# Other start addresses for the split weights and for every tile behind them, in a one-core decoder block

## The chip, the cores and the metric

The kernel runs on one core of one Trainium2 chip. The metric is the device time of one execution in microseconds (us); the times before the change are given as the median of three runs.

## The reference

One decoder block for 256 tokens of width 2048, in float32: a per-channel shift, scale and gate from `c`, a mixer made of sparse attention (NSA) beside a state-space layer (S5), and then a layer of 16384 single-neuron experts (PEER) of which each token uses 16 in each of 8 heads. Cut to what matters here:

```python
h = rms_norm(x, norm_mix_g[i]) * (1.0 + sc1) + sh1
proj = h @ w_in[i]
...
mixed = ga * (o_attn @ w_up_attn[i]) + gb * (y @ w_up_ssm[i])
x = x + g1 * (mixed @ w_out[i])
h2 = rms_norm(x, norm_ffn_g[i]) * (1.0 + sc2) + sh2
x = x + g2 * peer(h2, peer_w_q[i], peer_sub_keys[i], peer_u[i], peer_v[i])
```

In `peer`, the products of `h2` with `peer_u` are called the first expert products here, and those of the gated result with `peer_v` the second. The kernel forms both for all experts and gives the unused ones a gate of zero.

## The kernel before

**Split products.** Every large product is made of three float32r products. `load_split` (lines 95 to 101) loads a block of 128 x 1024 weights into `st`, ScalarE copies it, rounded, to `hi` (line 98), and VectorE writes the rest `st - hi` to `lo` (line 100). The activations are split in the same way by `split` (lines 103 to 105) into the two halves of a tile: `cat` for the projections (`hcat`), for `w_out` (`mcat`) and for queries and first expert products (`h2`); `ycat`, `y2cat` and `ocat` for the smaller products; `wcat` for the second expert products. Then `hi*hi`, `hi*lo` and `lo*hi` are summed in PSUM.

```python
    def load_split(src):
        st = load(src)
        hi = stream.tile([P, 1024], FR, name="hi", bufs=3)
        S.activation(hi, st, AF.Copy)
        lo = stream.tile([P, 1024], FR, name="lo", bufs=3)
        V.tensor_sub(lo, st, hi.bitcast(F32))
        return hi, lo
```

**Which operand stands still.** In the stages with lines 431 to 433 (`first_columns`, the first 24 blocks of `w_in`) and 512 to 514 (`pair_T`: the rest of `w_in`, `glu_w`, `w_up_ssm`, `w_up_attn`, the query weights and `peer_u`) a slice of 128 columns of `hi` or `lo` is loaded into the array, and 256 columns of the activations (`cat`, `ycat`, `y2cat` or `ocat`) move through it: 24 matmuls a load. In the stages with lines 529 to 531 (`cols_t`: `w_v` and `w_out`) and 1180 to 1182 (`v_cols`: `peer_v`) it is the other way round: 128 columns of `cat` or `wcat` are loaded, and 512 columns of `hi` or `lo` move: 12 matmuls a load. Of the 738 loads, 48 go to `first_columns`, 394 to `pair_T`, 40 to `cols_t` and 256 to `v_cols`.

```python
                    PE.matmul(pt[:, e], wh, c[:, 0], start=(k == 0), stop=False)
                    PE.matmul(pt[:, e], wh, c[:, 1], start=False, stop=False)
                    PE.matmul(pt[:, e], wl, c[:, 0], start=False, stop=(k == n - 1))
```

Each matmul loads its own 128 columns first; the load for the next matmul runs while this one's columns move (engines PEld and PE in the profile).

**Order.** `tick` mixes the small work (modulation vectors, S5, attention, top-16 searches) into the loads by tables of how many loads have gone by. The expert stage then goes through 16 groups of 8 expert blocks: per group 32 loads of `peer_v` and the `peer_u` products of the next group between them.

**Where tiles lie.** Pools take a row of each partition one behind the other: `const`, `stream`, `big`, then the pool of the stage. In `stream` these are five buffers of `st`, three of `hi`, three of `lo` (4096 bytes each); in `big` the tile `pad` (line 177, 48 floats) and `cat`; behind them `pa` or `pb` with all others. A tile named `t8` (`ycat`, `y2cat`, `ocat` and others) is 8256 bytes long, so that the next begins 64 bytes further modulo 512; a buffer of `wcat` (line 1161) is 8320 bytes long, so that the three are 128 bytes apart modulo 512. A buffer is taken by turns: the loads use `hi` and `lo` number 0, 1, 2, 0, and so on.

Of the kernel before, what the change touches and what calls it, by code (L numbers as in the profile page):

```python
# [11 lines left out]
F32 = mybir.dt.float32  # L12
FR = mybir.dt.float32r
# [7 lines left out]
P = 128  # L21
# [51 lines left out]
def hybrid_block(ctx: ExitStack, tc: tile.TileContext, i: dict, out: bass.AP):  # L73
# [4 lines left out]
    stream = ctx.enter_context(tc.tile_pool(name="stream", bufs=3))  # L78
    big = ctx.enter_context(tc.tile_pool(name="big", bufs=1))
# [10 lines left out]
    def load(src):  # L90
        st = stream.tile([P, 1024], F32, name="st", bufs=5)
        nc.sync.dma_start(st, src)
        return st

    def load_split(src):
        st = load(src)
        hi = stream.tile([P, 1024], FR, name="hi", bufs=3)
        S.activation(hi, st, AF.Copy)  # L98
        lo = stream.tile([P, 1024], FR, name="lo", bufs=3)
        V.tensor_sub(lo, st, hi.bitcast(F32))  # L100
        return hi, lo

# [71 lines left out]
        for tb in range(TB):  # L174
            V.tensor_scalar(dst[tb], xt[tb], r[:, tb:tb + 1], None, op0=OP.mult)

    big.tile([P, 48], F32, name="pad")

    def new_cat():
        return big.tile([P, KD, 2, SEQ], FR, name="cat")  # L180
# [266 lines left out]
    def stage(sn, order=None, after=None):  # L447
        ks, units, steps = stages[sn]
        sl = slice(ks[0], ks[-1] + 1)
        V.scalar_tensor_tensor(a1[:, sl], modT[:, 16 + ks[0]:17 + ks[-1]], 1.0, par("norm_mix_g")[:, sl],  # L450
                               op0=OP.add, op1=OP.mult)
        for k in ks[::2]:
            modulate_T(hcat, k, [t[:, 0] for t in xn], a1, modT[:, 0:16], mm_bank)
        for n, u in enumerate(order or range(len(units))):
            for step in steps[len(steps) * n // len(units):len(steps) * (n + 1) // len(units)]:
                step()
            if (sn, n) == (2, 0):
                bias_load()
            if (sn, n) == (2, 6):
                make_table(0)  # L460
            if (sn, n) == (3, 0):
                bias_rows()
            w = i["w_first0"][sn, u] if sn < 2 else i["w_first"][sn - 2, u]
            first_columns(*load_split(w), ks, units[u])
            if after:
                after(n)
# [34 lines left out]
    def pair_T(blocks, cat, kh):  # L501

        pt = mm_bank()
        for e, srcs in enumerate(blocks):
            n = len(srcs) * kh
            for h, src in enumerate(srcs):
                hi, lo = load_split(src)
                for kk in range(kh):
                    k = h * kh + kk
                    c = at(cat, k)  # L510
                    wh, wl = hi[:, kk * P:(kk + 1) * P], lo[:, kk * P:(kk + 1) * P]
# [3 lines that stand above are left out]
                tick()  # L515
        return pt

    def cols_t(srcs, cat, emit):

        pts = [ps_bank() for _ in range(TB)]  # L520
        for c, src in enumerate(srcs):
            hi, lo = load_split(src)
            for tb in range(TB):
                for kk in range(2):
                    k = 2 * c + kk
                    wh, wl = hi[:, kk * 512:(kk + 1) * 512], lo[:, kk * 512:(kk + 1) * 512]
                    sh = cat[:, k, 0, tb * P:(tb + 1) * P]
                    sl = cat[:, k, 1, tb * P:(tb + 1) * P]
                    PE.matmul(pts[tb], sh, wh, start=(k == 0), stop=False)
                    PE.matmul(pts[tb], sh, wl, start=False, stop=False)  # L530
                    PE.matmul(pts[tb], sl, wh, start=False, stop=(k == 2 * len(srcs) - 1))
            tick()
        for tb in range(TB):
            emit(tb, pts[tb])
# [833 lines left out]
```

## Time and profile before

| what | value |
|---|---|
| median of 3 runs | 2552.22 us (2546.16 to 2557.81) |
| the profiled execution's own time | 2554.16 us |
| its span, first to last instruction | 2552.1 us |
| PE busy, share of the span | 96% |
| weight loads (PEld) busy | 83% |
| VectorE busy | 65% |
| ScalarE busy | 46% |
| mean granted TensorE clock | 0.981 |

The busy share of PE counts a matmul from its start to its modelled end. Matmuls overlap in the array, so that the next one starts long before the end of this one; the time that a row of matmuls takes is read from start to start, and the duration of one is longer than that by the way through the array.

### The profile page before, as it was taken

Reading aid. Unit: us, or ns where it says so; the run is one execution under the profiler, and the core shown is the slowest. Engines: PE = TensorE matmul, PEld = TensorE weight load, DVE = VectorE, ACT = ScalarE, POOL = GpSimd, SP = SyncE. Lnnn points to the kernel's source line nnn. Section 1 sums busy time; section 2 is a strip of 40 time slices with the busy share of each in tenths; the row PEclk is TensorE's granted clock in tenths of the full one; section 3 lists DMA queues with packets and bytes.
Section 4 is the critical chain, followed back from the end, with each engine's and each line's share of the span. In section 5 each row is a group of like instructions: output and inputs, shape, how many; then the busy total and the mean of one; then the engine's idle time right before and its main releaser. Section 6 shows DMA issues by size and latency. Waiting matters only on the chain.

```text
span 2552.1 us, 42825 instructions
## 1 busy us (share of the span) xinstructions
PE 2448.5 (96%) x17410; PEld 2127.0 (83%) x17410; DVE 1668.6 (65%) x2690; ACT 1176.5 (46%) x1527; POOL 65.1 (3%) x117
## 2 busy tenths in 40 slices
PE   7999999999999999995599999999999999999997
PEld 4787787777898788995488999999899999989996
DVE  4559767886555579959555665666666566665666
ACT  4444524645534534456444444444444444444444
POOL 0000200000000000000100000000000000000000
PEclk9999999999999999996799999999999999999999
DMA  9965666666777677554756665665666566565554
GB/s 347 376 227 176 225 202 210 214 199 209 281 264 255 211 237 253 188 186 173 298 197 192 211 198 197 203 208 191 203 206 207 192 204 206 191 207 189 190 191 139
DMA packets 149761, 552.03 MB, mean 216 GB/s; under 512 B 16748, under 2 KB 20492, under 8 KB 147133
## 3 DMA queue, kind: packets, MB, share of 16 engines
q1 hardware_dynamic: 135200, 493.08, 57.1%
q0 software_dynamic: 8928, 40.17, 4.4%
q10 hardware_dynamic: 5436, 16.06, 1.8%
q8 instruction: 136, 2.23, 0.4%
q14 instruction: 61, 0.49, 0.1%
HBM read 526.12 MB, written 23.12 MB: 215 GB/s over the span
## 4 chain that ended last, share of the span: by engine, by line
PE 57%; DVE 5%; DMA 2%; ACT 1%; issue 1%; DVEq 0%; POOL 0%; POOLq 0%; ACTq 0%
PE mm L512 10%; PE mm L513 10%; PE mm L514 10%; PE ps L1182 9%; PE ps L1180 9%; PE ps L1181 9%; DVE o L1120 1%; DVE o L1122 1%; DMA st<-in_peer_w_q_dram 1%; DVE lo L100 1%; DVE o L1118 1%; DMA gm<-gt_dram 0%; ACT hi L98 0%; PE ps L1004 0%; DMA gt_dram<-stage 0%
## 5 line engine op out<-in xcount | busy, mean ns | idle before, releaser
L100 DVE TENSOR_TENSOR lo<-st,hi 128x1024 fp32r<-128x1024 f32 x738 | 902.2, 1223 | 667.9 <-ACT hi L98 666.8
L98 ACT ACTIVATE hi<-st 128x1024 fp32r<-128x1024 f32 x738 | 781.4, 1060 | 1120.3 <-PE mm L513 430.5
L512 PE MATMUL mm<-cat,hi 128*128 128x256 f32 x2832 | 804.1, 284 | 0.6 <-ACT cat L104 0.6
L513 PE MATMUL mm<-cat,hi 128*128 128x256 f32 x2832 | 793.8, 280 | 1.0 <-DVE cat L105 0.9
L514 PE MATMUL mm<-cat,lo 128*128 128x256 f32 x2832 | 792.8, 280 | 0.0
L512 PEld LDWEIGHTS mm<-cat,hi 128*128 128x128 f32 x2832 | 533.6, 188 | 33.4 <-issue 26.5
L514 PEld LDWEIGHTS mm<-cat,lo 128*128 128x128 f32 x2832 | 539.6, 191 | 1.6 <-issue 0.8
L513 PEld LDWEIGHTS mm<-cat,hi 128*128 128x128 f32 x2832 | 533.5, 188 | 5.9 <-issue 2.4
L1180 PE MATMUL ps<-hi,wcat 128*128 128x512 f32 x1024 | 401.7, 392 | 21.0 <-ACT wcat L104 21.0
L1182 PE MATMUL ps<-hi,wcat 128*128 128x512 f32 x1024 | 403.0, 394 | 0.2 <-DVE wcat L105 0.2
L1181 PE MATMUL ps<-lo,wcat 128*128 128x512 f32 x1024 | 401.3, 392 | 0.0
L1180 PEld LDWEIGHTS ps<-hi,wcat 128*128 128x128 f32 x1024 | 193.1, 189 | 60.7 <-ACT wcat L104 21.1
L1182 PEld LDWEIGHTS ps<-hi,wcat 128*128 128x128 f32 x1024 | 192.9, 188 | 46.4 <-DVE wcat L105 4.8
L1181 PEld LDWEIGHTS ps<-lo,wcat 128*128 128x128 f32 x1024 | 193.2, 189 | 40.6
L431 PE MATMUL ps<-cat,hi 128*128 128x256 f32 x384 | 110.9, 292 | 0.5 <-ACT hi L98 0.5
L433 PE MATMUL ps<-cat,lo 128*128 128x256 f32 x384 | 106.8, 284 | 1.0 <-DVE lo L100 1.0
L432 PE MATMUL ps<-cat,hi 128*128 128x256 f32 x384 | 107.3, 281 | 0.1
L222 PE MATMUL ps<-st,sct 128*32 128x256 f32 x960 | 88.8, 390 | 0.4 <-DMA st<-in_ada_w_dram 0.4
L431 PEld LDWEIGHTS ps<-cat,hi 128*128 128x128 f32 x384 | 72.7, 190 | 16.0 <-issue 12.6
L1128 PE MATMUL ps<-o,o 128*128 128x128 f16 x512 | 49.5, 281 | 38.1 <-DVE o L1120 38.0
L1128 PEld LDWEIGHTS <-o 128*128 128x128 f16 x512 | 46.5, 159 | 41.0 <-DVE o L1120 40.8
L433 PEld LDWEIGHTS ps<-cat,lo 128*128 128x128 f32 x384 | 71.9, 190 | 4.5 <-DVE lo L100 2.0
(353 smaller groups left out, 2606.3 us busy)
## 6 DMA issues: line engine op xcount, KB each, us to landing
st<-in_peer_u_dram SPq DMA_DIRECT2D x256, 512.0 KB, 4.0
st<-in_peer_v_dram SPq DMA_DIRECT2D x256, 512.0 KB, 4.2
st<-in_ada_w_dram SPq DMA_DIRECT2D x136, 512.0 KB, 4.4
st<-in_w_in_dram SPq DMA_DIRECT2D x66, 512.0 KB, 4.0
ada_w<-in_ada_w_dram SPq DMA_DIRECT2D x28, 1024.0 KB, 9.5
st<-in_w_first_dram SPq DMA_DIRECT2D x48, 512.0 KB, 6.0
st<-in_w_out_dram SPq DMA_DIRECT2D x32, 512.0 KB, 4.0
st<-in_peer_w_q_dram SPq DMA_DIRECT2D x32, 512.0 KB, 4.3
```

The costliest lines, as they stand in the source:

```text
L98: S.activation(hi, st, AF.Copy)
L100: V.tensor_sub(lo, st, hi.bitcast(F32))
L431: PE.matmul(pt[:, e], hi[:, cs], hcat[:, k, 0], start=first, stop=False)
L432: PE.matmul(pt[:, e], hi[:, cs], hcat[:, k, 1], start=False, stop=False)
L433: PE.matmul(pt[:, e], lo[:, cs], hcat[:, k, 0], start=False, stop=end)
L512: PE.matmul(pt[:, e], wh, c[:, 0], start=(k == 0), stop=False)
L513: PE.matmul(pt[:, e], wh, c[:, 1], start=False, stop=False)
L514: PE.matmul(pt[:, e], wl, c[:, 0], start=False, stop=(k == n - 1))
L1128: PE.matmul(pt[:, tt], o1[:, part, :, h0 + tt], o2[:, h0 + tt], start=(part == 0), stop=(part == 1))
L1180: PE.matmul(pts[tb], wc[:, 0, ts], vh, start=(eb == 0), stop=False)
L1181: PE.matmul(pts[tb], wc[:, 0, ts], vl, start=False, stop=False)
L1182: PE.matmul(pts[tb], wc[:, 1, ts], vh, start=False, stop=(eb == GRP - 1))
```

## The change

The tiles `hi` and `lo` get 32 bytes more (8 floats, not used); one tile `gap` of 416 bytes, not used, is taken between the first `hi` and the first `lo`; and `pad` shrinks from 192 to 160 bytes.

```diff
+    gaps = {}
+
     def load_split(src):
         st = load(src)
-        hi = stream.tile([P, 1024], FR, name="hi", bufs=3)
+        hi = stream.tile([P, 1024 + 8], FR, name="hi", bufs=3)[:, :1024]
         S.activation(hi, st, AF.Copy)
-        lo = stream.tile([P, 1024], FR, name="lo", bufs=3)
+        if "gap" not in gaps:
+            gaps["gap"] = stream.tile([P, 104], F32, name="gap", bufs=1)
+        lo = stream.tile([P, 1024 + 8], FR, name="lo", bufs=3)[:, :1024]
         V.tensor_sub(lo, st, hi.bitcast(F32))
         return hi, lo
...
-    big.tile([P, 48], F32, name="pad")
+    big.tile([P, 40], F32, name="pad")
```

No instruction is added, removed or moved: the built programs hold the same instructions in the same order on each engine, with the same waits and the same shapes, and only addresses differ. All tiles behind `lo` lie 576 bytes further (64 modulo 512). Start of the tiles in a partition, in bytes modulo 512, from the built programs:

| tile | before | with the change |
|---|---|---|
| `st`, 5 buffers | 0 | 0 |
| `hi`, buffers 0, 1, 2 | 0, 0, 0 | 0, 32, 64 |
| `lo`, buffers 0, 1, 2 | 0, 0, 0 | 0, 32, 64 |
| `cat` | 192 | 256 |
| `wcat`, buffers 0, 1, 2 | 0, 128, 256 | 64, 192, 320 |
| `ycat`, two tiles | 0, 448 | 64, 0 |
| `y2cat`, two tiles | 64, 128 | 128, 192 |
| `ocat`, two tiles | 256, 320 | 320, 384 |
| `xs`, `sq`, `acc` | 0 | 64 |

Slices that matmuls take of these tiles begin a multiple of 512 bytes after the tile's start, so the table holds for them too.

## Rows read from the trace of the kernel before

**Rows 1.** The page's parts 1 and 4: TensorE's busy time, share of the span and instructions; and the shares of the span in the chain that ended last, by engine.

```profile
PE 2448.5 (96%) x17410; PEld 2127.0 (83%) x17410; DVE 1668.6 (65%) x2690; ACT 1176.5 (46%) x1527; POOL 65.1 (3%) x117
...
PE 57%; DVE 5%; DMA 2%; ACT 1%; issue 1%; DVEq 0%; POOL 0%; POOLq 0%; ACTq 0%
```

**Rows 2.** Busy time of each engine in four stretches of the span (start and end in us, length; then busy us and instructions of PE, weight loads, DVE, ACT and POOL; granted TensorE clock; DMA share; GB/s). The first three hold all that stands ahead of the expert stage (the third is mostly the gate matrices), the last is the expert stage.

```profile
0.00:1000.00 1000.00, 968.60 (x7624) 780.89 (x7625) 667.83 (x1494) 456.53 (x725) 46.12 (x92) 0.99 0.70 243
1000.00:1150.00 150.00, 146.79 (x1277) 145.79 (x1275) 117.69 (x225) 74.59 (x88) 0.52 (x1) 1.00 0.58 190
1150.00:1250.00 100.00, 45.11 (x448) 42.35 (x448) 77.03 (x57) 56.06 (x59) 6.99 (x11) 0.68 0.51 206
1250.00:2552.00 1302.00, 1287.99 (x8064) 1157.97 (x8064) 806.02 (x917) 589.29 (x658) 11.50 (x13) 0.99 0.60 199
```

**Rows 3.** Groups of instructions of the whole run by line and shape: line, engine, operation, out<-in, shapes, count, then busy us, mean ns of one, and the idle time before them with what ended it.

```profile
L100 DVE TENSOR_TENSOR lo<-st,hi 128x1024 fp32r<-128x1024 f32 x738 | 902.2, 1223 | 667.9 <-ACT hi L98 666.8
L512 PE MATMUL mm<-cat,hi 128*128 128x256 f32 x2832 | 804.1, 284 | 0.6 <-ACT cat L104 0.6
...
L98 ACT ACTIVATE hi<-st 128x1024 fp32r<-128x1024 f32 x738 | 781.4, 1060 | 1120.3 <-PE mm L513 430.5 <-PE ps L1182 288.8 <-issue 100.1
...
L431 PE MATMUL ps<-cat,hi 128*128 128x256 f32 x384 | 110.9, 292 | 0.5 <-ACT hi L98 0.5
```

**Rows 4.** Who waited for whom over the whole run (us in total, times, longest).

```profile
ACT hi L98 <- PE mm L513: 430.5, 260, 4.6
ACT hi L98 <- PE ps L1182: 288.8, 191, 2.1
```

**Rows 5.** Groups of TensorE in the expert stage alone, 1250 to 2552 us; columns as in rows 3.

```profile
L514 PE MATMUL mm<-cat,lo 128*128 128x256 f32 x1664 | 464.6, 279 | 0.0
...
L1181 PE MATMUL ps<-lo,wcat 128*128 128x512 f32 x1024 | 401.3, 392 | 0.0
```

**Rows 6.** The same for 1000 to 1150 us, the queries and the first expert products.

```profile
L513 PE MATMUL mm<-cat,hi 128*128 128x256 f32 x395 | 110.9, 281 | 0.0
```

**Rows 7.** The same for 350 to 600 us, the projections.

```profile
L513 PE MATMUL mm<-cat,hi 128*128 128x256 f32 x402 | 112.4, 280 | 0.0
```

**Rows 8.** TensorE's instructions in order of time, 1391 to 1397 us (start us, us, engine, line, operation, out<-in, shapes, count): the first and the last of 48 matmuls of an expert product that follow each other without a gap.

```profile
1391.34 0.28 PE L512 MATMUL mm<-cat,hi 128*128 128x256 f32 x1
...
1396.66 0.28 PE L514 MATMUL mm<-cat,lo 128*128 128x256 f32 x1
```

**Rows 9.** The same view, 1479 to 1485 us: the first and the last of 48 matmuls of a later expert product.

```profile
1479.04 0.28 PE L512 MATMUL mm<-cat,hi 128*128 128x256 f32 x1
...
1484.57 0.28 PE L514 MATMUL mm<-cat,lo 128*128 128x256 f32 x1
```

**Rows 10.** The groups of TensorE in 1391.4 to 1396.6 us and in 1479.1 to 1484.5 us (one row of each, in this order), columns as in rows 3.

```profile
L513 PE MATMUL mm<-cat,hi 128*128 128x256 f32 x16 | 4.4, 276 | 0.0
...
L513 PE MATMUL mm<-cat,hi 128*128 128x256 f32 x16 | 4.5, 281 | 0.0
```

**Rows 11.** TensorE in order of time, 757.6 to 759.1 us, in the product with `w_up_attn`: the first matmul on `ocat`'s first tile and the first on its second tile, 12 intervals later.

```profile
757.62 0.29 PE L512 MATMUL mm<-ocat,hi 128*128 128x256 f32 x1
...
759.06 0.28 PE L512 MATMUL mm<-ocat,hi 128*128 128x256 f32 x1
```

**Rows 12.** The same view, 756.3 to 757.5 us: two matmuls on `ocat`'s second tile, ten intervals apart.

```profile
756.32 0.28 PE L513 MATMUL mm<-ocat,hi 128*128 128x256 f32 x1
...
757.50 0.28 PE L514 MATMUL mm<-ocat,lo 128*128 128x256 f32 x1
```

**Rows 13.** The same view, 631.2 to 633.1 us, in the product with `glu_w`: a matmul on `ycat`'s first tile, the first on its second tile (five intervals later), and the twelfth on that.

```profile
631.24 0.28 PE L513 MATMUL mm<-ycat,hi 128*128 128x256 f32 x1
...
631.84 0.29 PE L512 MATMUL mm<-ycat,hi 128*128 128x256 f32 x1
...
633.11 0.28 PE L514 MATMUL mm<-ycat,lo 128*128 128x256 f32 x1
```

**Rows 14.** The same view, 1339.1 to 1346.9 us, second expert products on the `wcat` buffers at 0 and 256: two matmuls 34 intervals apart.

```profile
1339.13 0.39 PE L1180 MATMUL ps<-hi,wcat 128*128 128x512 f32 x1
...
1346.84 0.39 PE L1181 MATMUL ps<-lo,wcat 128*128 128x512 f32 x1
```

**Rows 15.** The same view, 1347.5 to 1352.5 us, on the `wcat` buffer at 128: two matmuls 21 intervals apart.

```profile
1347.54 0.40 PE L1181 MATMUL ps<-lo,wcat 128*128 128x512 f32 x1
...
1352.42 0.40 PE L1181 MATMUL ps<-lo,wcat 128*128 128x512 f32 x1
```

**Rows 16.** The same view, 1438.6 to 1440.5 us, on the `wcat` buffer at 256 just after TensorE had stood still (the row ahead of these lasts 0.50 us): two matmuls eight intervals apart.

```profile
1438.62 0.40 PE L1180 MATMUL ps<-hi,wcat 128*128 128x512 f32 x1
...
1440.49 0.40 PE L1182 MATMUL ps<-hi,wcat 128*128 128x512 f32 x1
```

**Rows 17.** The same view, 800 to 803.2 us, in the product with `w_out`: two matmuls 14 intervals apart.

```profile
799.97 0.39 PE L529 MATMUL ps<-hi,cat 128*128 128x512 f32 x1
...
803.17 0.39 PE L531 MATMUL ps<-hi,cat 128*128 128x512 f32 x1
```

**Rows 18.** The splits into `wcat` on ScalarE and VectorE, whole run, columns as in rows 3.

```profile
L105 DVE TENSOR_TENSOR wcat<-xs,wcat 128x512 fp32r<-128x512 f32 x64 | 43.3, 685 | 2.2 <-ACT wcat L104 2.2
...
L104 ACT ACTIVATE wcat<-xs 128x512 fp32r<-128x512 f32 x64 | 39.7, 625 | 24.2 <-DVE xs L1159 20.7 <-PE ps L1182 3.4
```

## Prediction

> **What bounds the kernel now.** I began with the busy shares and the chain that ended last: TensorE is busy for 96% of the span, and its matmuls are the largest part of the chain by far [rows 1]. By stretches that holds nearly everywhere: 969 of the first 1000 us, 147 of the 150 us after, 1288 of 1302 us in the expert stage; only from 1150 to 1250 us, where the gate matrices are built, is TensorE idle for half the time, and almost none of the split products lie there [rows 2]. Who waits for whom says the same from the other side: ScalarE's rounding of the weights waits for matmuls to give a buffer back, 430 and 289 us in total [rows 4]. So the end is set by how closely matmuls follow each other, and the change, which alters addresses alone, can act only through that, or through the work of other engines on the moved tiles.
>
> The next view is the order of time on TensorE, read from start to start. Matmuls of the same form, with no gap between them, run at several steady rates:
>
> - 256 columns, moving from `cat` (192) against `hi` and `lo` (0): 48 matmuls start within 1391.34 to 1396.66 us, 47 intervals of 113.2 ns [rows 8]; another product of the same kind takes 47 intervals of 117.7 ns from 1479.04 to 1484.57 us [rows 9]. The mean duration is 276 ns in the one and 281 ns in the other [rows 10], so a duration is the interval plus 163 ns. That lets me read intervals from mean durations.
> - 256 columns, moving from `ocat`'s first tile (256) against weights at 0: 12 intervals take 1.44 us, 120.0 ns each [rows 11]; from its second tile (320): 118.0 ns [rows 12].
> - 256 columns, moving from `ycat`: 120.0 ns on the tile at 0; on the tile at 448 the first eleven intervals take 1.27 us, 115.5 ns each [rows 13].
> - 512 columns from `hi` and `lo` (0) against `wcat`: 226.8 ns on the buffers at 0 and 256 [rows 14], 232.4 ns on the buffer at 128 [rows 15]; on the one at 256, right after TensorE had stood still, 233.8 ns [rows 16].
> - 512 columns against `cat` (192): 228.6 ns [rows 17].
>
> I put these in order by one number, the start of the moving tile less that of the stationary one, modulo 256, and call it the distance. Then 0 and 256 give the same 120.0, 64 and 320 about 118, and 192 and 448 both can reach about 113. With 512 columns, distance 0 gives 226.8 while its rhythm lasts. This order is my reading of the rows; they show it only for multiples of 64.
>
> **The change part by part.** *Other engines.* VectorE's subtraction takes 1223 ns for 1024 columns, ScalarE's copy 1060 ns [rows 3]; the same operations with 512 columns into `wcat`, which lies at 0, 128 and 256, take 685 and 625 ns [rows 18], so the further 512 columns cost 1.05 and 0.85 ns each and the start of the output shows no price of its own. I cost the moved outputs at nothing. The cover is that both engines wait for TensorE [rows 4] and are busy for 65% and 46% of the span [rows 1]. If VectorE's 738 subtractions became 100 ns longer, the 74 us would still fit into its idle 35%. `st`, which the weight loads write, does not move.
>
> *256 columns against `hi` and `lo`.* `cat` goes to 256, the weights to 0, 32 and 64 by turns: distances 0, 224 and 192, each for 24 matmuls. Distance 0 has its row: 120.0 ns, entry included [rows 11]. For 192 I take what `ycat` shows on entry from distance 0, 1.27 us for eleven intervals [rows 13], and 113.2 ns for the other 13: 114.3 ns. Distance 224 has no row. It lies between 192 and 0, so it is bounded by 113.2 and 120.0; I take 117.2, a little above the middle, since it is entered from 0 each time. The mean is (120.0 + 117.2 + 114.3) / 3 = 117.2 ns. Now it is 279 - 163 = 116 ns for the 4992 matmuls of the expert stage [rows 5], 281 - 163 = 118 ns for some 1190 between 1000 and 1150 us [rows 6], and about 117 ns for the other 3470 on `cat`, taken from the projections' 280 [rows 7]. That gives 4992 x 1.2 = +6.0 us, 1190 x -0.8 = -1.0 us and 3470 x 0.2 = +0.7 us: **+5.7 us**. The 960 matmuls on `ycat`, `y2cat` and `ocat` change places among the same prices: 0, with 3 us either way.
>
> *512 columns against `wcat`.* The moving tile is at 0, 32 or 64 now, `wcat` at 64, 192 or 320. For the two buffers at 64 and 320 the distances are 192, 224 and 0, for the one at 192 they are 64, 96 and 128. Each load has 12 matmuls and then the distance changes, so the rhythm of 226.8 ns that now lasts over loads and buffers [rows 14] is broken every time. I bound the first two buffers by 226.8 and by the 233.8 after a break [rows 16] and take the middle, 230.3; for the third I take the middle of 228.6 [rows 17] and 232.4 [rows 15], 230.5. The mean, 230.4, stands against 392 - 163 = 229 ns now [rows 5]: 3072 x 1.4 = **+4.3 us**. The 480 matmuls of `cols_t` get distances 0, 32 and 64 in place of one price of 228.6; bounded by 226.8 and 233.8, I take +1 ns: **+0.5 us**.
>
> The sum is +10.5 us on the profiled execution's 2554.2 us. That execution is 1.9 us above the median of the runs, so on the median I forecast 2552.2 + 10.5 = 2562.7, say **2563 us**. TensorE being the bound, none of it is hidden except between 1000 and 1250 us.
>
> *The bounds of the sum.* Lowest: 192 and 224 at 113.2, 0 at 120.0, mean 115.5: 4992 x -0.5 - 1190 x 2.5 - 3470 x 1.5 = -10.7 us; 512 columns at (2 x 226.8 + 228.6) / 3 = 227.4: -4.9 us; the small terms -4 us; together -20 us, 2533 us. Highest: all 256-column matmuls at 120.0: 4992 x 4 + 1190 x 2 + 3470 x 3 = +33 us; 512 columns at 233.8: +15 us; small terms +5 us; together +53 us, 2605 us.
>
> **A rule that says otherwise.** The rows show one and the same instruction at 113.2, 117.7 and 120.0 ns on tiles that differ in where they start [rows 8, 9, 11]. The Trainium skill, "TensorE: Matmul & The Clock Gate", section "Step-by-step: what each phase is for", has it that TensorE reads moving and stationary operands through two independent ports, and that loading the next weights takes nothing from the running matmul. By that rule the addresses would not matter, and the change would cost nothing; the trace does not agree as far as these rates go. I keep it as a rival.
>
> **The rivals.**
>
> *No effect, 2552 us.* The rates could belong to something else than the start addresses: 113.2 and 117.7 ns occur at one and the same pair of addresses [rows 8, 9], and so do 226.8 and 233.8 [rows 14, 16]. Then the mixture stays as it is and the sum is 0. Against it: the buffer at 128 and the tiles at 256 have prices of their own [rows 11, 15]. Chance 0.16.
>
> *Slower: the rhythm is lost everywhere.* The mechanism is that a fast rate needs one distance for many loads, as in rows 8 and 14, and a shift by 32 after each load prevents it. Then 192 stays at 117.7, 224 costs 120.0 as 0 does, mean 119.2: 4992 x 3.2 + 1190 x 1.2 + 3470 x 2.2 = +25 us; `wcat` at (2 x 233.8 + 230.5) / 3 = 232.7: 3072 x 3.7 = +11.4 us; `cols_t` +1.5 us. Together +38 us, 2590 us. With the other terms as forecast, this side begins (over 0.5%, 12.8 us, about what a measurement of this kernel can tell from no change) where distance 224 costs more than some 118 ns. For it: the rate after a break [rows 16]. Against it: `ycat` falls to its fast rate within a load [rows 13]. Chance 0.21.
>
> *Faster: the shifts break the slow rhythm instead.* If each new distance throws the matmuls into the fast rate, as rows 13 show for one, all of them would come to about 114 ns: 4992 x -2 - 1190 x 4 - 3470 x 3 = -25 us, and -5 us from 227.4 ns on `wcat`: 2522 us. Against it: `ocat` at distance 0 keeps 120.0 ns [rows 11], and 0 is the distance of every third load. Chance 0.13.
>
> **How the numbers follow.** The forecast, a mixture, has 0.50: +10.5 us with some 10 us either way, so about 0.33 of it within 0.5% and 0.17 slower by more. With no effect (0.16) that makes 0.49 within, 0.17 + 0.21 = 0.38 slower, 0.13 faster. The range goes from 2540 us (20 us above the faster rival's middle) to 2584 us (most of the way to the slower rival): what lies outside are most of the faster rival and the upper half of the slower one, some 0.2.
>
> **What would show it.** In the order of time, loads on `hi` number 0 should run at 120 ns against `cat`, those on number 2 near 114 ns, with number 1 between; the mean duration of line 514 in the expert stage should be near 280 ns (279 now), that of line 1181 near 393 (392 now), and no long stretch at 389. ScalarE's and VectorE's durations should stay at 1060 and 1223 ns. The prediction is wrong if intervals below 113 or 226 ns appear, for no row here has them; if the rates do not follow the buffer's number; or if ScalarE or VectorE becomes what matmuls wait for.

## The result, and the profile after

The kernel with the change takes 2577.79 us (median of four runs, 2576.32 to 2581.93) against 2550.76 us for the kernel before in the runs beside it (2546.16 to 2557.81): ratio 1.0106, 95% interval 1.0079 to 1.0133, 27 us slower. The forecast was 2563 us with 2540 to 2584 around it. So the time lies in the range and the sign of the sum was right, but the sum, +10.5 us, was two and a half times too small, and the case "slower by over 0.5%", which came true, had had 0.38.

The page's busy times and the shares of the chain that ended last, against [rows 1]:

```profile
PE 2479.9 (96%) x17410; PEld 2146.6 (83%) x17410; DVE 1669.2 (65%) x2690; ACT 1177.3 (46%) x1527; POOL 64.9 (3%) x117
...
PE 57%; DVE 5%; DMA 2%; ACT 1%; issue 1%; DVEq 0%; POOL 0%; SPq 0%; ACTq 0%; POOLq 0%
```

Only TensorE's column moved: +31.4 us for the same 17410 matmuls, and +19.6 us of weight loads beside them. The profiled execution's span is 2579.9 us against 2552.1. The four stretches, with the columns of [rows 2] (the first three have the same bounds; the last is the expert stage again, to the later end):

```profile
0.00:1000.00 1000.00, 970.60 (x7563) 782.39 (x7564) 662.19 (x1460) 455.98 (x723) 45.93 (x92) 1.00 0.70 242
1000.00:1150.00 150.00, 149.99 (x1273) 148.10 (x1271) 119.45 (x255) 68.82 (x80) 0.52 (x1) 1.00 0.59 193
1150.00:1250.00 100.00, 51.33 (x514) 48.07 (x512) 81.12 (x59) 63.66 (x67) 6.98 (x11) 0.67 0.46 190
1250.00:2580.00 1330.00, 1308.00 (x8064) 1168.03 (x8064) 806.48 (x918) 588.81 (x658) 11.48 (x13) 0.99 0.60 197
```

The granted clock is what it was in every stretch, within 0.01. The expert stage holds the same 8064 matmuls and costs 1308.0 - 1288.0 = 20.0 us more. The other 11.4 us of busy time lie ahead of it, where the first 1000 us now see 61 matmuls fewer get done. Of the 31.4 us the span shows 27.8; the other 3.6 us were taken in by time in which TensorE stood idle.

The groups behind that, with the columns of [rows 3, 5]: first VectorE's and ScalarE's work on the moved tiles (whole run; what were lines 100, 98, 105 and 104).

```profile
L104 DVE TENSOR_TENSOR lo<-st,hi 128x1024 fp32r<-128x1024 f32 x738 | 902.6, 1224 | 684.4 <-ACT hi L100 678.8 <-PE ps L795 3.7 <-PE mm L518 1.3
...
L100 ACT ACTIVATE hi<-st 128x1024 fp32r<-128x1024 f32 x738 | 782.1, 1061 | 1144.2 <-PE mm L517 453.4 <-PE ps L1186 264.5 <-issue 141.6
...
L109 DVE TENSOR_TENSOR wcat<-xs,wcat 128x512 fp32r<-128x512 f32 x64 | 43.4, 685 | 2.3 <-ACT wcat L108 2.3
...
L108 ACT ACTIVATE wcat<-xs 128x512 fp32r<-128x512 f32 x64 | 39.2, 617 | 24.7 <-DVE xs L1163 21.2 <-PE ps L1186 3.4
```

Then TensorE in the expert stage:

```profile
L518 PE MATMUL mm<-cat,lo 128*128 128x256 f32 x1664 | 467.5, 281 | 0.0
...
L1185 PE MATMUL ps<-lo,wcat 128*128 128x512 f32 x1003 | 395.9, 395 | 0.0
```

And in the projections, 350 to 600 us, and in the queries and first expert products, 1000 to 1150 us (one row of each view):

```profile
L517 PE MATMUL mm<-cat,hi 128*128 128x256 f32 x392 | 110.7, 283 | 0.0
```
```profile
L517 PE MATMUL mm<-cat,hi 128*128 128x256 f32 x410 | 115.4, 282 | 0.0
```

The outputs on shifted addresses cost the other engines nothing: 1224 and 1061 ns for 1223 and 1060, 685 for 685. TensorE's matmuls are longer everywhere: in the expert stage 279 became 281 and 392 became 395 [rows 5], in the projections 280 became 283 [rows 7], between 1000 and 1150 us 281 became 282 [rows 6].

One expert product, in order of time: the first matmul of each of its four loads of 24, and the matmul behind the last (columns as in [rows 8]).

```profile
1362.32 0.28 PE L516 MATMUL mm<-cat,hi 128*128 128x256 f32 x1
...
1365.06 0.28 PE L516 MATMUL mm<-cat,hi 128*128 128x256 f32 x1
...
1367.89 0.28 PE L516 MATMUL mm<-cat,hi 128*128 128x256 f32 x1
...
1370.77 0.28 PE L516 MATMUL mm<-cat,hi 128*128 128x256 f32 x1
...
1373.60 0.40 PE L1184 MATMUL ps<-hi,wcat 128*128 128x512 f32 x1
```

By the addresses of the built program these four loads lie in `hi` and `lo` number 2, 1, 0, 2: numbered by address, the loads take the buffers in the order 0, 2, 1, not 0, 1, 2 as said ahead of the prediction. So the distances of `cat` follow each other as 0, 192, 224, and only 192 is entered from 0. The steps are 2.74, 2.83, 2.88 and 2.83 us, over 24 intervals 114.2, 117.9, 120.0 and 117.9 ns. So the rate does follow the buffer, as forecast: 120 on number 0, 118 on number 1. But number 2 is fast in the first load of this product only, and slow when it comes right behind number 0.

### The profile page after: what moved, and what is told of

The parts are those of the page before. It is cut to its first block, busy times and chain, and to the rows that moved or that the text cites. A ratio compares the mean times of both kernels' runs of the same rounds, so it can differ in the third digit from the quotient of the medians.

```text
span 2579.9 us, 42825 instructions
## 1 busy us (share of the span) xinstructions
PE 2479.9 (96%) x17410; PEld 2146.6 (83%) x17410; DVE 1669.2 (65%) x2690; ACT 1177.3 (46%) x1527; POOL 64.9 (3%) x117
## 4 chain that ended last, share of the span: by engine, by line
PE 57%; DVE 5%; DMA 2%; ACT 1%; issue 1%; DVEq 0%; POOL 0%; SPq 0%; ACTq 0%; POOLq 0%
PE mm L517 10%; PE mm L516 10%; PE mm L518 10%; PE ps L1186 9%; PE ps L1184 9%; PE ps L1185 9%; DVE o L1124 1%; DVE o L1126 1%; DMA st<-in_peer_w_q_dram 1%; DVE lo L104 1%; DVE o L1122 1%; DMA gm<-gt_dram 0%; PE ps L1008 0%; ACT hi L100 0%; DMA gt_dram<-stage 0%
## 5 line engine op out<-in xcount | busy, mean ns | idle before, releaser
L104 DVE TENSOR_TENSOR lo<-st,hi 128x1024 fp32r<-128x1024 f32 x738 | 902.6, 1224 | 684.4 <-ACT hi L100 678.8
L100 ACT ACTIVATE hi<-st 128x1024 fp32r<-128x1024 f32 x738 | 782.1, 1061 | 1144.2 <-PE mm L517 453.4
```

## The experiments

Three theories stood at the start. **Distance**: the interval depends on where the moving tile starts less where the stationary one starts, modulo 256 bytes, with a price for each distance. **Place**: it depends on where a tile lies by itself. **Rhythm**: the fast rates need one and the same distance for many loads, and the turning of the buffers, not their distances, costs the time. Each experiment but the last was timed in three rounds beside the kernel before, whose median was 2550.3 to 2552.8 us there; ratios are to those runs, with a 95% interval, and can differ by 0.15% from the quotient of the medians. In all of them the instructions are those of the kernel before, on other addresses.

**Only the shift of the tiles.** `hi` and `lo` stay at 0; everything behind lies where the change puts it.

```diff
-    big.tile([P, 48], F32, name="pad")
+    big.tile([P, 64], F32, name="pad")
```

> All tiles behind the weights lie 64 bytes further, as in the change (cat at 256, wcat at 64, 192, 320), but hi and lo stay at 0 in all buffers. Distance theory (a matmul's interval is set by the start of its moving tile less that of its stationary one, modulo 256): every 256-column matmul on cat is at distance 0 and runs at 120.0 ns, as on ocat's first tile before; 9648 x (120.0 - 116.6) = +33 us, and some +2 ns on 3072 second expert matmuls, +6 us: about 2590 us (2583 to 2600), slower than the change itself. Rhythm theory (it is the turning of distances with the weight buffers that costs): nothing turns here, 2551 us. Place theory (the new places of cat and wcat cost by themselves): as the change, 2578 us.

2590.76 us, ratio 1.0140 (1.0122 to 1.0158). Half of the change is slower than the whole of it. The expert stage of this kernel:

```profile
L516 PE MATMUL mm<-cat,lo 128*128 128x256 f32 x1664 | 470.8, 283 | 0.0
...
L1183 PE MATMUL ps<-lo,wcat 128*128 128x512 f32 x1024 | 404.2, 395 | 0.0
```

283 ns is 163 more than 120, on every load: `cat` at 256 against weights at 0 is the dear distance 0.

**Only the staggered buffers.** `hi` and `lo` at 0, 32, 64; `cat`, `wcat` and the rest where they were.

```diff
-        hi = stream.tile([P, 1024], FR, name="hi", bufs=3)
+        hi = stream.tile([P, 1024 + 8], FR, name="hi", bufs=3)[:, :1024]
...
+            gaps["gap"] = stream.tile([P, 104], F32, name="gap", bufs=1)
...
-    big.tile([P, 48], F32, name="pad")
+    big.tile([P, 24], F32, name="pad")
```

> hi and lo at 0, 32 and 64 as in the change, but cat back at 192 and wcat at 0, 128, 256. Distance theory: distances 192, 160, 128 for 256 columns, about 114 to 118 ns, mean 117, +4 us; 0, 32, 64 on two wcat buffers and 128, 160, 192 on the third, about 231 ns, +6 us: about 2561 us (2553 to 2568). Rhythm theory: about as slow as the change, 2578 us. Place theory: 2551 us.

2569.68 us, ratio 1.0055 (1.0035 to 1.0074): between the 2561 of the distances and the 2578 of the rhythm, and outside the 2553 to 2568 that I gave the distances. The sum behind the 2561 was too small in the same places as the prediction's: from start to start the projections went from 115.1 to 117.3 ns (+7.6 us) and the second products from 228.9 to 231.7 (+8.5 us). So this kernel alone does not decide between distance and rhythm. One of its expert products, the first matmul of each of four loads and of the fifth:

```profile
1415.44 0.28 PE L516 MATMUL mm<-cat,hi 128*128 128x256 f32 x1
...
1418.18 0.28 PE L516 MATMUL mm<-cat,hi 128*128 128x256 f32 x1
...
1421.01 0.28 PE L516 MATMUL mm<-cat,hi 128*128 128x256 f32 x1
...
1423.86 0.29 PE L516 MATMUL mm<-cat,hi 128*128 128x256 f32 x1
...
1426.60 0.28 PE L516 MATMUL mm<-cat,hi 128*128 128x256 f32 x1
```

The distances of these loads are 192, 128, 160 and 192, the intervals 114.2, 117.9, 118.8 and 114.2 ns. Here distance 192 is fast again in the fourth load, behind a load at 160; in the kernel with the change, behind a load at 0, it was not. This holds beyond the two products: taken over the whole run, from the starts of the matmuls and the addresses of the program, all 77 loads at 192 right behind a load at 0 have intervals of 117.7 to 117.9 ns there, and 62 of 74 right behind one at 160 are fast here.

**All tiles shifted by the same 64 bytes**, the weights too (one unused tile of 16 floats ahead of `hi`).

```diff
+            gaps["gh"] = stream.tile([P, 16], F32, name="gh", bufs=1)
```

> hi and lo at 64 in all buffers, cat at 256, wcat at 64, 192, 320: every tile at its place in the change, but every distance as it was before. Distance theory and rhythm theory: 2551 us, expert stage with the same mean durations as before (279 ns for line 514's products, 392 ns for line 1181's). Place theory: 2578 us.

2551.71 us, ratio 0.9998 (0.9987 to 1.0009). `hi`, `lo` and every tile behind them lie elsewhere, and nothing changes; the middle line of its expert stage keeps the 279 ns. The place theory falls.

```profile
L517 PE MATMUL mm<-cat,hi 128*128 128x256 f32 x1664 | 464.8, 279 | 0.0
```

**`lo` alone moved by 256 bytes** against everything else (a gap of 64 floats between `hi` and `lo`, `pad` at 112, so that all behind stays).

> lo lies at 256 in all buffers and hi at 0; cat stays at 192, wcat at 0, 128, 256. If distances count modulo 256: nothing changes, 2551 us within 5 us, and lo's matmuls keep hi's intervals. If they count modulo 512: lo's third of the matmuls gets other distances, the intervals of hi and lo part, and the time moves by more than 5 us.

2551.95 us, ratio 0.9999 (0.9985 to 1.0012): 256 bytes do not count. The matmuls that move against `lo` keep the 279 ns of those on `hi`, so distances matter modulo 256.

```profile
L518 PE MATMUL mm<-cat,lo 128*128 128x256 f32 x1664 | 464.6, 279 | 0.0
```

**`hi` and `lo` all at 32**, other tiles as in the change: the distances of its buffers number 1 (224 for `cat`, 224 and 96 for `wcat`, 32 in `cols_t`), but without turning.

```diff
+            gaps["gh"] = stream.tile([P, 8], F32, name="gh", bufs=1)
...
-    big.tile([P, 48], F32, name="pad")
+    big.tile([P, 56], F32, name="pad")
```

> hi and lo at 32 in all buffers, cat at 256, wcat at 64, 192, 320: the distances that buffer number 1 has in the change, held for every load (224 for 256 columns; 224, 96, 224 for wcat). Distance theory: the prices of that buffer in the change hold without any turning, 118.1 ns for 256 columns, 233.3 ns for wcat, 232.4 ns for cols_t: 9648 x 2.1 + 3072 x 4.3 + 480 x 3.5 = +35 us, 2586 us (2580 to 2594), and the mean of this one, of the kernel with all weights at 0 (2590.8 us) and of the one with all at 64 (2551.7 us) comes to the change's 2578 us. Rhythm theory: held distances settle into faster rates than turning ones, below 2570 us, and the mean of the three stays well below the change.

2583.72 us, ratio 1.0129 (1.0113 to 1.0146). In its expert stage:

```profile
L516 PE MATMUL mm<-cat,hi 128*128 128x256 f32 x1664 | 467.5, 281 | 0.0
...
L1185 PE MATMUL ps<-lo,wcat 128*128 128x512 f32 x1024 | 405.9, 396 | 0.0
```

With one steady distance the rates are as slow as with three. That refutes the rhythm as the main cause. The three kernels with steady distances of which the change is made up (weights at 0, 32, 64 against the shifted tiles: 2590.8, 2583.7, and 2551.7 for the third, whose distances are those of the kernel with everything shifted) have a mean of 2575.4 us; the change takes 2577.8. So the distances account for some 23 to 25 of the 27 us. The 2 us that are left to turning by these times, or 4 us by the ratios (mean 1.0089 against 1.0106), are within the uncertainty of the times.

**One distance for `wcat`.** Three kernels with the weights at 0 and `cat` at 192, and all `wcat` buffers at one distance, to price it and to see whether the rate of the second products sets how the first ones start (an entry theory: 113 ns after any rate but the locked 227).

```diff
+            if not wcat:
+                pool.tile([P, 48], F32, name="wpad")
-            w = pool.tile([P, 4 * 2 * SEQ + 32], FR, name="wcat", bufs=3)[:, :8 * SEQ]
+            w = pool.tile([P, 4 * 2 * SEQ + 64], FR, name="wcat", bufs=3)[:, :8 * SEQ]
```

(48 floats: all 64 bytes from the weights; 32 floats: 128; without the `wpad` tile: 0.)

> Otherwise the kernel before; the three wcat buffers at 192, 448, 192, so that every second expert matmul has distance 64 (229 to 230 ns in rows on other stages). Entry theory (whether a first expert product at distance 192 runs at 113 or 118 ns is set by the rate of the matmuls just ahead: 118 after the locked 226.7 ns, 113 after any other): all first expert products run at 113.4 ns, -13 us, and wcat costs +2 us: about 2540 us. If the rate is not set by what is ahead: 40% at 113 ns as before, 2554 us.

2550.5 us, ratio 0.9988 (0.9969 to 1.0008); its ten runs spread widely, from 2536.84 to 2561.5.

> Otherwise the kernel before; the three wcat buffers at 0, 256, 0, all at distance 0. Second expert matmuls run at about 227 ns, -7 us. Entry theory: all first expert products come after the locked rate and run at 117.7 ns, +7 us: 2551 us. If the rate is not set by what is ahead: 2544 us.

2550.45 us, ratio 1.0001 (0.9987 to 1.0015). The time is the 2551 of the entry theory and not the 2544 of the other answer. But the rows of its profile, taken in its shortest execution (2543.49 us), are not the theory's: from start to start the first products run at 116.9 ns in the mean, with a fifth of them fast, where it wanted 117.7 throughout and the kernel before has 116.2.

> Otherwise the kernel before; the three wcat buffers at 128, 384, 128, all at distance 128. Second expert matmuls run at 232.5 ns, +11 us. Entry theory: all first expert products run at 113.4 ns, -13 us: 2549 us. If the rate is not set by what is ahead: 2562 us.

2564.74 us, ratio 1.0048 (1.0032 to 1.0065). The middle line of the second products in these three, in the same order:

```profile
L1185 PE MATMUL ps<-lo,wcat 128*128 128x512 f32 x1024 | 403.6, 394 | 0.0
```
```profile
L1183 PE MATMUL ps<-lo,wcat 128*128 128x512 f32 x1018 | 396.6, 390 | 0.0
```
```profile
L1185 PE MATMUL ps<-lo,wcat 128*128 128x512 f32 x1024 | 405.3, 396 | 0.0
```

The distance prices the second products (390, 394, 396 ns at 0, 64, 128). It does not decide the first ones by itself: they have the same mean, 280 ns, in all three. Two products of the last kernel, one after the other, 1354 to 1365 us and 1387 to 1398 us, with the same distances ahead of them:

```profile
L516 PE MATMUL mm<-cat,lo 128*128 128x256 f32 x31 | 8.6, 277 | 0.0
```
```profile
L516 PE MATMUL mm<-cat,lo 128*128 128x256 f32 x31 | 8.7, 281 | 0.0
```

One is fast, the next slow. The entry theory falls as it stands: the rate of the products just ahead does not set the rate by itself. It is not without influence, though. In the profile of the kernel before, the first expert products that come behind second products on the `wcat` buffer at 128 are fast in 18 of 20 cases, those behind one at 0 or 256 in 1 of 32; in the second profile of it, below, in 18 of 20 and 2 of 32. With all of `wcat` at one distance that order by buffers is gone.

**Other places for `cat`**, against weights at 0, all else kept: 32, 96, 160.

```diff
-    big.tile([P, 48], F32, name="pad")
+    big.tile([P, 40], F32, name="pad")
...
+    big.tile([P, 8], F32, name="pad2")
```

(40 and 8 floats for 160; 24 and 24 for 96; 72 and 40 for 32, `pad2` behind `cat`.)

> Kernel before with only cat moved from 192 to 32 modulo 256: all 9652 matmuls of 256 columns on cat get the distance 32, cols_t the distance 224 (233.5 ns in place of 229: +2 us); wcat and the other tiles keep their distances. No run has shown the distance 32 for 256 columns. If only the distances 192 and 448 have a fast rate and every other distance costs 118 to 120 ns: +13 to +33 us and the 2, 2566 to 2586 us. If there is a second fast distance (113.3 ns throughout): 2552 - 32 + 2 = 2522 us.

2560.29 us, ratio 1.0032 (1.0018 to 1.0046): neither of the two answers. Most of its intervals are 116 and 117 ns, cheaper than the 118 that I had as the lower bound of a slow distance, and no product is fast throughout.

> The same with cat at 96: distance 96, cols_t at 160 (233.9 ns, +2 us). Bounds as for 32: 2566 to 2586 us if every distance but 192 costs 118 to 120 ns; 2522 us if 96 is a fast one.

2584.25 us, ratio 1.0132 (1.0107 to 1.0158).

> The same with cat at 160, distance 160 throughout, which cost 118.6 ns where the buffers stood in turn. If the price belongs to the distance whatever the load before had: 4992 x 2.6 + 1190 x 0.6 + 3470 x 1.6 = +19 us, and +2 us in cols_t: 2573 us. If a distance that stays the same for many loads can fall to a faster rate, as 192 does: down to 2522 us.

2576.31 us, ratio 1.0103 (1.0073 to 1.0132). The rows of these three in the expert stage:

```profile
L517 PE MATMUL mm<-cat,lo 128*128 128x256 f32 x1664 | 464.1, 279 | 0.0
```
```profile
L517 PE MATMUL mm<-cat,lo 128*128 128x256 f32 x1664 | 468.4, 282 | 0.0
```
```profile
L517 PE MATMUL mm<-cat,lo 128*128 128x256 f32 x1664 | 467.3, 281 | 0.0
```

At 160 the price is the one of the turning buffers (118.7 ns, there 118.6), so steadiness does not make it cheaper. No place tried for `cat` beats 192, where it was.

**The kernel before, profiled again.**

> The kernel before itself, profiled once more: is the share of expert products of 256 columns that run at 113 ns in place of 118 the same from one execution to the next? If addresses and order of instructions set it alone, the same products are the fast ones, and the mean duration of line 514 in the expert stage is 279 ns again, that of the products' first row near 1391 us 276. If something outside the program decides it, other products are fast, and that mean may lie anywhere from 276 to 281 ns.

2555.47 us in one run. The mean in the expert stage is 279 ns again, and of its 39 unbroken rows of one or two products 36 have the same rate in both executions. Three differ; one of them, 1441 to 1451 us in the first profile, is 1443 to 1453 us in the second:

```profile
L512 PE MATMUL mm<-cat,hi 128*128 128x256 f32 x30 | 8.3, 276 | 0.0
```
```profile
L512 PE MATMUL mm<-cat,hi 128*128 128x256 f32 x31 | 8.7, 281 | 0.0
```

Between 1000 and 1150 us more differs: four of the twelve products there are fast in the second execution and slow in the first, and the mean is 279 ns for the 281 of [rows 6].

```profile
L513 PE MATMUL mm<-cat,hi 128*128 128x256 f32 x400 | 111.7, 279 | 0.0
```

So the program sets most of which product is fast in the expert stage, but not all of it, and less ahead of it.

The prices together, in ns from start to start: means of all intervals without a gap (under 150 ns for 256 columns, under 300 for 512), in the expert stage where the distance occurs there, each matmul matched with the addresses of its two tiles in the built program, from the kernels in which the distance holds for most matmuls of that form (for 64 with 256 columns, from the smaller products of the kernel before; for 32 and 160 with 512 columns, from `cols_t` of two experiments; for 128 with 256 columns, from the staggered kernel):

```
distance         0      32      64      96     128     160     192     224
256 columns  119.9   116.7   118.0   120.0   118.4   118.7   116.2   118.3
512 columns  227.2   233.3   229.2   233.5   232.4   234.2   233.4   233.4
```

116.2 at distance 192 is a mixture of products at 113.4 and at 117.8 ns. Where distances turn, a price can be another: 0 with 512 columns costs 230.0 in the kernel with the change.

## Why the prediction was right in sign and short in size

**What bounds the kernel** stood: only TensorE's spacing changed, and the end moved with it. *Other engines* at nothing was right [rows 18]. That the rates go by distance modulo 256 was right too, shown by the two kernels that move tiles without changing a distance (0.9998, 0.9999). The forecast's price for distance 0, 120.0 [rows 11], measured 119.6.

The range held the time, but the forecast's own mixture did not: it had some 10 us either way around 2563, and 2577.8 is 15 us above. The range held because it was drawn most of the way to the slower rival.

**What failed are in the main sizes, in three terms.** The sum was +10.5 us, the span grew by 27.8; the misses below come to some 21 us, less the 3.6 us of added busy time that idle time took in. All of them point the same way, so none made up for another.

1. *The present rate of the projections* (3470 matmuls, forecast +0.2 ns). I took 117 ns from the mean duration of 280 [rows 7] by taking off the 163 ns of [rows 10]. From start to start the intervals there are 115.0 ns. The 163 was read in an unbroken product; in the projections other work lies between, and the few matmuls beside it, whose durations are stretched to as much as 394 ns, raise the mean duration. Between 350 and 600 us 36 of 51 loads ran at the fast rate, as the one behind this list does, with 22 intervals of 113.6 ns; with the change 9 of 49 do. The intervals went to 117.9 (the duration from 280 to 283): 2.7 ns more than forecast, +9.4 us if it holds for all 3470, the largest miss. The queries and first products next to it (282 for 281, forecast -0.8) add about 2 us.
2. *512 columns against `wcat`* (forecast 230.4, +4.3 us). Distances 192 and 224 cost 232.7 and 233.3 in the kernel with the change, where I took 230.3 as a middle of 226.8 and 233.8; the third buffer's 64, 96 and 128 came to 231.0, 233.4 and 232.9 against 230.5, and 0 stayed at 230.0. The mean is 232.2 against 228.9 before: +10.2 us, 5.8 more than forecast. The 233.8 ns of [rows 16], which I read as a price after a break, is near what most distances cost at all times.
3. *256 columns at distance 192* (forecast 114.3, from `ycat`'s entry [rows 13]). It cost 117.1 in the expert stage. `ycat` gets from distance 0 to 192 by changing the moving tile and becomes fast; here the stationary tile changes, and behind a load at 0 none of 77 loads was fast. That step, the entry of one stage carried to another, is the one place where the mechanism failed and not only a size. The prediction also had 224 entered from 0; it comes behind 192. With 224 at 118.1 for 117.2, the expert products lost about 4 us more than forecast.

The load of item 1 in order of time, the second and the last of its 24 matmuls, in the kernel before (columns as in [rows 8]):

```profile
436.14 0.28 PE L513 MATMUL mm<-cat,hi 128*128 128x256 f32 x1
...
438.64 0.28 PE L514 MATMUL mm<-cat,lo 128*128 128x256 f32 x1
```

**The rivals.** *No effect* is refuted by the shift of tiles alone (1.0140). The Trainium skill, "TensorE: Matmul & The Clock Gate", section "Step-by-step: what each phase is for", has the two operands read through independent ports, with loading the next weights taking no read bandwidth from the running matmul. By that rule, as the prediction reads it, the kernels with other start addresses would all take the time of before; these runs do not agree, as the same instructions cost up to 1.4% more. *Slower* (2590 us) gave 117.7 for distance 192 and 232.7 for `wcat`, and both came true within 0.6 ns. But its cause is not what the runs show: steady distances (2583.7, 2590.8, 2584.3 us) are as slow as turning ones, and 224 costs 118.1, not the 120.0 it wanted. Turning itself costs something with 512 columns, most at the distance 0 on `wcat`, 230.0 in place of 227.2, and at 192 behind a load at 0. *Faster* is refuted; though in the staggered kernel the turning does hold distance 192 at 114.7 ns in the mean, the other two distances it must visit cost 118.4 and 118.6.

**What stays open.** Why the distance has a price at all: the runs show the price, not which accesses get in each other's way. And what sets a product at distance 192 to 113.4 or to 117.8 ns. In the expert stage the rate is there from its first matmuls and kept over 96 or 192 of them; it is mostly the same from execution to execution; the distance of the products ahead goes with it in the kernel before, but does not set it alone. That a load at distance 0 ahead prevents the fast rate is seen in the rows of the change alone, and no kernel was run to isolate it. The same choice may be behind the spread of single runs (2536.8 to 2561.5 us with all of `wcat` at 64), which was not shown.

## What to carry to other kernels

Where matmuls stand back to back, list for each pair of operands the start of the moving tile less that of the stationary one, modulo 256 bytes, and read the interval of each from start to start in the trace: here they cost 116 to 120 ns and 227 to 234 ns, and a shift of unused bytes moved the whole kernel by up to 1.4%. A stagger of rotating buffers averages the prices of all the distances it passes through, so it pays only if none of them is dear; here one steady distance for each form (192 for 256 columns, 0 for 512) took 2550.45 us, less than the stagger's 2569.68 at the same `cat`, but no less than the kernel before. Take the present rate from starts, stage by stage, not from a mean duration less a constant that was read in another stage.

## What the runs showed of the hardware that was not expected

- The interval between float32r matmuls of the same shape depends on the relative start of their operands, with a period of 256 bytes: 116.2 to 120.0 ns with 256 columns, 227.2 to 234.2 with 512, and the cheapest distance for one is among the dear ones for the other.
- At distance 192 there are two steady rates, 113.4 and 117.8 ns, for the same instructions on the same addresses within one execution, and some products run at the other rate in the next execution: 3 of 39 rows of products in the expert stage, 4 of 12 products between 1000 and 1150 us.
